# Gate/up products of a decoder layer: two more k tiles by seven products in most groups, one weight sum made by adding transfers, one partial product put into a PSUM bank

## The chip, the cores and the metric

The kernel runs on one core of a Trainium2 chip. The metric is device time in microseconds from the first to the last instruction of one execution. Several executions are timed and the median is given.

## The reference

One decoder layer on 256 tokens with 2048 channels, all in float32: a SwiGLU feed-forward block (FFN) at half weight, a token mixer (latent attention beside differential attention, merged by gates), a second such FFN, with a layer norm after each. What the change touches is the first half of both FFNs, the gate and up products:

```python
D_MODEL, SEQ, D_FF = 2048, 256, 5632
def _swiglu(x, w_gate, w_up, w_down):
    return (jax.nn.silu(x @ w_gate) * (x @ w_up)) @ w_down
...
h = _layer_norm(ALPHA * h + 0.5 * _swiglu(h, ffn1_w_gate[l], ffn1_w_up[l], ffn1_w_down[l]), ln1_g[l], ln1_b[l])
mix = _mixer(h, ...)
h = _layer_norm(ALPHA * h + mix, ln2_g[l], ln2_b[l])
h = _layer_norm(ALPHA * h + 0.5 * _swiglu(h, ffn2_w_gate[l], ffn2_w_up[l], ffn2_w_down[l]), ln3_g[l], ln3_b[l])
```

## The kernel before, in words

**Products.** Every float32 operand is split into a high part (a cast to fp32r on ScalarE, line 149) and a low part (the operand less the high part, a subtraction on VectorE, line 150). A product of a 128 x 128 block of activations with a 128 x 512 block of weights is then three matmuls, high by high, high by low and low by high (`triple`, lines 202 to 204), into one PSUM bank of 128 x 512.

**Units.** Weights stream from HBM in tiles of 128 x 1024, which hold two k tiles (of 128 rows) by 512 columns. One tile is a *unit*: its load is issued by SyncE, its split is written into a pair of tiles from a ring (`next_pair`), and its matmuls follow. `unit`, `advance` and `look` set how far these run apart: with `look(3, 4)` three units are loaded ahead of the one that is split, and four are split ahead of the one that is multiplied. The ring has six pairs in the gate/up stage (`set_ring(6)` in `second`, ten pairs before). The weights of plain units land in four rotating buffers `raw`.

**The FFN** (`ffn`, lines 705 to 821). The gate and up weights are interleaved, so that a column block of 512 holds 256 gate and 256 up columns; there are 22 such blocks, and 16 k tiles (numbered 0 to 15). The first two blocks are done by `project` with plain products (stage "projection" in this text). Then `Hybrid` does ten *groups* of two column blocks, w0 and w1, for both halves of the tokens (b = 0 and 1).

**Hybrid.** In a group the k tiles 0 to 7 are taken as a 2 x 2 matrix of blocks (tokens by k tiles 0-3 and 4-7, and these by w0 and w1), which is multiplied by seven block products in place of eight (a Strassen-like scheme). The activation sums and their splits are made once per FFN by `Seven`. The weight sums are made in each group: `plan` names for every product the block that is loaded, the tile that is split, and the tile that is first added to it on VectorE (line 344, for products 5, 6, 7 and 4). The blocks are called "11" and "21" (w0, k tiles 0-3 and 4-7), "12" and "22" (w1). Each of the seven is two units with one bank, 6 matmuls a unit. The k tiles 8 to 15 are plain units, four for each column block, 12 matmuls a unit (`plain`). The products go into banks X, Z, Y, W; what several outputs share is copied out by ScalarE in between (`after`, n1 to n3 and q5, tiles `snap`) and added or subtracted by VectorE at the end of an output (`sum_done`, line 728), followed by SiLU on ScalarE (line 715) and the gate product on VectorE (line 719). The order of units in a group is written out by hand: product 1, a plain unit, 5, plain, 6, plain, 7, plain, 2, plain, 4, plain, 3, plain, plain.

**After a group**, two units later (`later(2, ...)`), `turn_out` transposes the rows of h in blocks on VectorE (line 606), and GpSimd issues the stores (line 608) and later the loads (`get_h`, line 736) of the turned rows for the down product, done by `Sliced`.

**What sets the order.** Each engine works through a queue of its own in order. A scheduler at build time turns the program into these queues by priorities and its own estimate of times, and places tiles into slots as they come free: the large tiles (ring, `sraw`, `snap`, splits of activations) share 40 slots (`SLOTS`, tag "act"), the small ones six (`tmp_tile`). So the order of instructions on an engine need not be that of the source, and a tile that gets its slot later moves what follows. The same `Hybrid` serves the mixer with `small=True`.

Of the kernel before, what the change touches and what calls it, by code (L numbers as in the profile page):

```python
# [11 lines left out]
F32 = mybir.dt.float32  # L12
# [6 lines left out]
P = 128  # L19
# [3 lines left out]
KD = D // P  # L23
# [7 lines left out]
G = 2  # L31
SLOTS = 40
LAG = 5
# [26 lines left out]
def layer_kernel(ctx: ExitStack, tc: tile.TileContext, a: dict, out: bass.AP):  # L60
# [188 lines left out]
    class Seven:  # L249
# [35 lines left out]
        def minus(self):  # L285
# [10 lines left out]
            V.scalar_tensor_tensor(out=lo, in0=a0, scalar=-1.0, in1=hi.bitcast(F32), op0=ALU.mult, op1=ALU.subtract)  # L296

    class Hybrid:


        def __init__(self, x, seven, k_tiles, small=False):

            self.x, self.seven, self.k_tiles = x, seven, k_tiles
            self.raws = {n: [act_tile([P, 1024], F32, "sraw") for _ in range(2)] for n in ("11", "12", "22")}
            self.raws["21"] = self.raws["12"] if small else [act_tile([P, 1024], F32, "sraw") for _ in range(2)]
            self.snaps = [[act_tile([P, 2, 512], F32, "snap") for _ in range(2)] for _ in range(1 if small else 2)]
            self.last = (3, 2, 4) if small else (2, 4, 3)
            self.turn = 0

        def group(self, w0, w1, done):  # L310
            banks = {}
            snap = [t[:, i, :] for t in self.snaps[self.turn % len(self.snaps)] for i in range(2)]
            self.turn += 1
            n1, n2, n3, q5 = snap
            R = self.raws
# [11 lines left out]
            def bank(n):  # L327
# [3 lines left out]
                return banks[n], first  # L331

            def seventh(p, s):
                load_block, src, add, b = plan[p]
                st = {}

                def load():
                    w, j0 = blocks[load_block]
                    nc.sync.dma_start(R[load_block][s], w[j0 + s])

                def prep():
                    t = R[src][s]
                    if add is not None:
                        V.tensor_tensor(out=t, in0=t, in1=R[add[1]][s], op=ALU.add)  # L344
                    pair = next_pair()
                    split(*pair, t)
                    st["pair"] = [v.rearrange("p (g n) -> p g n", g=G) for v in pair]

                def now():
                    o, first = bank(b)  # L350
                    wh, wl = st["pair"]
                    xh, xl = self.seven.at_[p]
                    for g in range(G):
                        k = 2 * s + g
                        triple(o, xh[:, k, :], xl[:, k, :], wh[:, g, :], wl[:, g, :], first and g == 0,
                               s == 1 and g == 1 and p in stops, b in "XZ")
                    if s == 1 and p in after:
                        after[p]()
                unit(load if load_block else None, prep, now)

            def plain(n, j, last=False):
# [13 lines left out]
                def now():  # L375
                    wh, wl = st["pair"]
                    for b in range(2):
                        o, first = bank(names[b])
                        for g in range(G):
                            k = 2 * j + g  # L380
                            triple(o, self.x.at(0, k, b), self.x.at(1, k, b), wh[:, g, :], wl[:, g, :],
                                   first and g == 0, last and g == 1, n == 1)
                    if last:
                        done(1, 0, banks["Z"], n2, ALU.add)
                        done(1, 1, banks["X"], q5, ALU.add)
                unit(load, prep, now)

            end = self.k_tiles // G - 1
            for p, n, j in zip((1, 5, 6, 7) + self.last, (0, 0, 0, 0, 1, 1, 1), (4, 5, 6, 7, 4, 5, 6)):
                for s in range(2):  # L390
                    seventh(p, s)
                plain(n, j)
            plain(1, end, True)

# [310 lines left out]
    def ffn(n, x, wgu, wdn, residual, g, bt, each, first=None, between=None, nxt=None, cols=None):  # L705
# [19 lines left out]

        def sum_done(c, b, bank, snap, op):
            t = tmp_tile([P, 512], "gus")
            V.tensor_tensor(out=t, in0=bank, in1=snap, op=op)
            half(c, b, t[:, 256:512], t[:, 0:256])
# [16 lines left out]

        seven = Seven(x.raws)

        def second(j):
# [451 lines left out]

    xq = Acts(KD, "x", (0, 1))

# [117 lines left out]
```

## Time and profile before

| | |
|---|---|
| median of three runs | 1981.97 us (1980.86 to 1984.72) |
| profiled execution, first to last instruction | 1981.9 us |
| TensorE (PE) busy | 1967.9 us, 8832 instructions |
| VectorE (DVE) busy | 1770.4 us, 2089 instructions |
| ScalarE (ACT) busy | 1247.6 us |
| GpSimd (POOL) busy | 248.8 us |
| moved by DMA | 460.50 MB, mean 232 GB/s |
| of that, queue of GpSimd (q0) | 69.29 MB |

The records span the whole execution, so that the profiled execution has no time beside its span. The two gate/up stages (groups only) lie at about 50 to 490 us and 1330 to 1730 us; the down product of the first FFN follows until about 700 us, then the mixer. TensorE's busy times are modelled: a matmul of 512 columns is shown as 0.39 us, but the next starts 0.226 us after it. For the same reason the duration of an instruction on VectorE is longer than the distance to the next one. "DMA share" in a table by windows is the mean busy share of the 16 DMA engines, "idle before" the time in which an engine had nothing to run, with the instruction that ended it behind an arrow.

### The profile page before, as it was taken

Reading aid. Unit: us, or ns where it says so; the run is one execution under the profiler, and the core shown is the slowest. Engines: PE = TensorE matmul, PEld = TensorE weight load, DVE = VectorE, ACT = ScalarE, POOL = GpSimd, SP = SyncE. Lnnn points to the kernel's source line nnn. Section 1 sums busy time; section 2 is a strip of 40 time slices with the busy share of each in tenths; the row PEclk is TensorE's granted clock in tenths of the full one; section 3 lists DMA queues with packets and bytes.
Section 4 is the critical chain, followed back from the end, with each engine's and each line's share of the span. In section 5 each row is a group of like instructions: output and inputs, shape, how many; then the busy total and the mean of one; then the engine's idle time right before and its main releaser. Section 6 shows DMA issues by size and latency. Waiting matters only on the chain.

```text
span 1981.9 us, 25344 instructions
## 1 busy us (share of the span) xinstructions
PE 1967.9 (99%) x8832; PEld 1628.9 (82%) x8832; DVE 1770.4 (89%) x2089; ACT 1247.6 (63%) x1571; POOL 248.8 (13%) x463
## 2 busy tenths in 40 slices
PE   9999999999999999999999999999999999999997
PEld 7888888888888888888888888888888888888886
DVE  7999999999799889999877676799999999998986
ACT  6666666666556566666667764566666666665552
POOL 0111101012010011002223130001011100121000
PEclk9999999999999999999999999999999999999999
DMA  8667766658678666677667667657676666596763
GB/s 323 220 212 237 262 211 202 218 199 313 232 228 274 204 221 246 220 245 250 228 215 249 228 225 264 220 208 242 225 257 229 201 216 228 186 327 225 256 222 125
DMA packets 133649, 460.50 MB, mean 232 GB/s; under 512 B 19424, under 2 KB 19472, under 8 KB 133520
## 3 DMA queue, kind: packets, MB, share of 16 engines
q1 hardware_dynamic: 109296, 389.59, 57.4%
q0 software_dynamic: 24224, 69.29, 11.2%
q8 instruction: 69, 1.13, 0.2%
q14 instruction: 60, 0.49, 0.1%
HBM read 429.97 MB, written 28.84 MB: 231 GB/s over the span
## 4 chain that ended last, share of the span: by engine, by line
PE 90%; DVE 4%; DMA 3%; issue 2%; ACT 1%; SPq 0%; POOL 0%; DVEq 0%; ACTq 0%; POOLq 0%
PE mm L203 29%; PE mm L204 29%; PE mm L202 29%; DVE wring L150 2%; DMA raw<-in_dn_dram 1%; PE tr L203 1%; PE tr L204 1%; PE tr L202 1%; ACT wring L149 1%; DVE sraw L344 0%; PE tr L571 0%; DMA hraw<-hT 0%; DMA raw<-in_wgd_dram 0%; DMA raw<-in_gu_dram 0%; DVE sraw L519 0%
## 5 line engine op out<-in xcount | busy, mean ns | idle before, releaser
L149 ACT CAST wring<-raw 128x1024 fp32r<-128x1024 f32 (+2 forms) x499 | 516.2, 1039 | 338.7 <-PE mm L204 236.6
L150 DVE TENSOR_TENSOR wring<-raw,wring 128x1024 fp32r<-128x1024 f32 (+2 forms) x499 | 596.7, 1202 | 117.0 <-ACT wring L149 110.3
L149 ACT CAST wring<-sraw 128x1024 fp32r<-128x1024 f32 x436 | 453.7, 1052 | 217.4 <-PE mm L204 98.1
L150 DVE TENSOR_TENSOR wring<-sraw,wring 128x1024 fp32r<-128x1024 f32 x436 | 523.6, 1217 | 35.2 <-ACT wring L149 31.0
L204 PE MATMUL mm<-wring,h 128*128 128x512 f32 (+2 forms) x1296 | 499.3, 386 | 0.0
L203 PE MATMUL mm<-wring,h 128*128 128x512 f32 (+2 forms) x1296 | 498.5, 385 | 0.3 <-DVE wring L150 0.3
L202 PE MATMUL mm<-wring,h 128*128 128x512 f32 (+2 forms) x1296 | 498.6, 385 | 0.0
L203 PE MATMUL mm<-wring,xs 128*128 128x512 f32 x776 | 302.3, 390 | 0.3 <-DVE wring L150 0.3
L202 PE MATMUL mm<-wring,xs 128*128 128x512 f32 x776 | 302.5, 390 | 0.0
L204 PE MATMUL mm<-wring,xs 128*128 128x512 f32 x776 | 302.1, 389 | 0.0
L204 PEld LDWEIGHTS mm<-wring,h 128*128 128x128 f32 x1296 | 243.5, 188 | 48.9 <-DVE h L150 1.4
L202 PEld LDWEIGHTS mm<-wring,h 128*128 128x128 f32 x1296 | 243.5, 188 | 48.8 <-ACT h L149 1.0
L203 PEld LDWEIGHTS mm<-wring,h 128*128 128x128 f32 x1296 | 243.5, 188 | 48.7 <-DVE wring L150 0.9
L344 DVE TENSOR_TENSOR sraw<-sraw,sraw 128x1024 f32<-128x1024 f32 x208 | 249.9, 1211 | 1.6 <-DMA sraw<-in_gu_dram 1.5
L608 POOL DMA_DIRECT2D hT<-blocks x176 | 95.7, 551 | 766.5 <-DVE blocks L606 711.5
L203 PEld LDWEIGHTS mm<-wring,xs 128*128 128x128 f32 x776 | 145.7, 188 | 31.5 <-DVE wring L150 1.6
L202 PEld LDWEIGHTS mm<-wring,xs 128*128 128x128 f32 x776 | 145.7, 188 | 31.1 <-ACT snap L321 0.7
L204 PEld LDWEIGHTS mm<-wring,xs 128*128 128x128 f32 x776 | 145.7, 188 | 30.1
L203 PE MATMUL mm<-wring,x 128*128 128x512 f32 x384 | 149.6, 390 | 0.6 <-DVE wring L150 0.6
L202 PE MATMUL mm<-wring,x 128*128 128x512 f32 x384 | 149.5, 390 | 0.3 <-ACT wring L149 0.3
L204 PE MATMUL mm<-wring,x 128*128 128x512 f32 x384 | 149.3, 389 | 0.0
L203 PEld LDWEIGHTS mm<-wring,x 128*128 128x128 f32 x384 | 72.1, 188 | 16.2 <-DVE wring L150 1.3
(268 smaller groups left out, 1921.2 us busy)
## 6 DMA issues: line engine op xcount, KB each, us to landing
raw<-in_gu_dram SPq DMA_DIRECT2D x191, 512.0 KB, 4.4
sraw<-in_gu_dram SPq DMA_DIRECT2D x160, 512.0 KB, 5.2
raw<-in_dn_dram SPq DMA_DIRECT2D x140, 512.0 KB, 4.6
sraw<-in_dn_dram SPq DMA_DIRECT2D x36, 512.0 KB, 5.3
hraw<-hT POOLq DMA_DIRECT2D x68, 256.0 KB, 5.7
raw<-in_w_out_dram SPq DMA_DIRECT2D x32, 512.0 KB, 4.4
raw<-in_wgd_dram SPq DMA_DIRECT2D x24, 512.0 KB, 4.6
hT<-blocks POOLq DMA_DIRECT2D x176, 64.0 KB, 2.3
```

The lines of the kernel that those rows point to most:

```text
L149: S.copy(hi, src)
L150: V.tensor_tensor(out=lo, in0=src, in1=hi.bitcast(F32), op=ALU.subtract)
L202: PE.matmul(o, xh, wh, start=first, stop=False, skip_group_check=again)
L203: PE.matmul(o, xh, wl, start=False, stop=False, skip_group_check=again)
L204: PE.matmul(o, xl, wh, start=False, stop=last, skip_group_check=again)
L344: V.tensor_tensor(out=t, in0=t, in1=R[add[1]][s], op=ALU.add)
L608: nc.gpsimd.dma_start(to.rearrange("(g r) (i f) -> i r g f", g=4, i=4)[i], t[32 * i:32 * (i + 1), :].rearrange("r (g f) -> r g f", g=4))
```

## The change

Three things, all in `Hybrid` (FFNs only, not `small`):

1. In the groups p = 1, 2, 4, 5, 7, 8 and 10 of each FFN ("wide") the k tiles 8 and 9 are multiplied by the same seven products, as a 2 x 2 matrix with one k tile to a block: each product gets a third unit, half as wide (128 x 512, 3 matmuls), into the same bank, and one plain unit of either column block goes. The groups p = 3, 6 and 9 ("narrow") keep plain units there. The activation forms for it are made once per FFN (`Extra`), from a third kept quad of activations.
2. The sum for product 7, "12" + "22", is no longer an addition on VectorE. GpSimd issues a transfer that reads block "22" from HBM once more and adds it to the tile of "12".
3. Product 1 is put negated by ScalarE into the bank Y from bank X, where it lies; Y then accumulates on it, so that the output of Y needs no subtraction and no n1. The snaps are single in place of double, the order of units is a string, with another order for wide groups, and the slots are 41.

```diff
-SLOTS = 40
+SLOTS = 41
...
+    class Extra:
+        def __init__(self, x, q):
+            self.at_ = {}
+            self.x, self.q = x, q
+
+        def make(self):
+            raw = self.x.raws[self.q]
+            a0, a1, c0, c1 = (raw[:, b, i * P:(i + 1) * P] for i in range(2) for b in range(2))
+            f = tmp_tile([P, 2, 2, P], "fe")
+            fa, fb = f[:, 0], f[:, 1]
+            for out, in0, in1 in ((fa[:, 0], a1, c1), (fb[:, 0], a1, a0), (fa[:, 1], a0, fa[:, 0]), (fb[:, 1], c0, fa[:, 1])):
+                V.tensor_tensor(out=out, in0=in0, in1=in1, op=ALU.subtract)
+            t = act_tile([P, 2, 2, 2, P], F32R, "xe")
+            split(t[:, 0], t[:, 1], f)
+            for i, pair in enumerate(((5, 6), (7, 3))):
+                for m, p in enumerate(pair):
+                    self.at_[p] = [t[:, w, i, m] for w in range(2)]
+            k = 4 * self.q
+            for b, p in enumerate((2, 4)):
+                self.at_[p] = [self.x.at(w, k + 1, b) for w in range(2)]
+            t = act_tile([P, 2, P], F32R, "xm")
+            hi, lo = t[:, 0, :], t[:, 1, :]
+            S.mul(hi, a0, -1.0)
+            V.scalar_tensor_tensor(out=lo, in0=a0, scalar=-1.0, in1=hi.bitcast(F32), op0=ALU.mult, op1=ALU.subtract)
+            self.at_[1] = [hi, lo]
...
-            self.snaps = [[act_tile([P, 2, 512], F32, "snap") for _ in range(2)] for _ in range(1 if small else 2)]
-            self.last = (3, 2, 4) if small else (2, 4, 3)
-            self.turn = 0
-
-        def group(self, w0, w1, done):
+            if extra is not None:
+                for pair in (("11", "12"), ("22", "21")):
+                    t = act_tile([P, 2, 512], F32, "eraw")
+                    for i, n in enumerate(pair):
+                        self.raws[n] = self.raws[n] + [t[:, i, :]]
+            self.snaps = [act_tile([P, 2, 512], F32, "snap") for _ in range(2)]
+
+        def group(self, w0, w1, done, wide=False):
             banks = {}
-            snap = [t[:, i, :] for t in self.snaps[self.turn % len(self.snaps)] for i in range(2)]
-            self.turn += 1
-            n1, n2, n3, q5 = snap
+            small = self.small
+            n2, n3, q5, n1 = [t[:, i, :] for t in self.snaps for i in range(2)]
...
+            def begin():
+                S.mul(bank("Y")[0], banks["X"], -1.0)
+            if not small:
+                after[1] = begin
+                after[2] = lambda: done(0, 0, banks["Y"], None, None)
+
+            end_s = 2 if wide else 1
+
+            def source(name, s):
+                w, j0 = blocks[name]
+                if s < 2:
+                    return w[j0 + s]
+                i = j0 // 2
+                return w[4][:, i * 512:(i + 1) * 512]
...
                 def prep():
                     t = R[src][s]
-                    if add is not None:
+                    if add is not None and (small or p != 7):
                         V.tensor_tensor(out=t, in0=t, in1=R[add[1]][s], op=ALU.add)
-                    pair = next_pair()
+                    if not small and p == 6:
+                        nc.gpsimd.dma_start(R["12"][s], source("22", s), accum_op=ALU.add)
+                    pair = [v[:, :tiles * 512] for v in next_pair()]
                     split(*pair, t)
...
-                    for g in range(G):
-                        k = 2 * s + g
-                        triple(o, xh[:, k, :], xl[:, k, :], wh[:, g, :], wl[:, g, :], first and g == 0,
-                               s == 1 and g == 1 and p in stops, b in "XZ")
+                    for g in range(tiles):
+                        if s < 2:
+                            xh, xl = (v[:, 2 * s + g, :] for v in self.seven.at_[p])
+                        else:
+                            xh, xl = self.extra.at_[p]
+                        triple(o, xh, xl, wh[:, g, :], wl[:, g, :], first and g == 0,
+                               s == end_s and g == tiles - 1 and p in stops, b in "XZ" or not small)
...
-            for p, n, j in zip((1, 5, 6, 7) + self.last, (0, 0, 0, 0, 1, 1, 1), (4, 5, 6, 7, 4, 5, 6)):
-                for s in range(2):
-                    seventh(p, s)
-                plain(n, j)
-            plain(1, end, True)
+            if small:
+                order = "1p5p6p7p3q2q4qq"
+            elif wide:
+                order = "15p6pp72q4q3q"
+            else:
+                order = "15p6pp7p2q4q3qq"
+            turn = {n: iter(range(5 if wide else 4, end + 1)) for n in range(2)}
+            for i, c in enumerate(order):
+                if c in "pq":
+                    plain("pq".index(c), next(turn["pq".index(c)]), i == len(order) - 1)
+                else:
+                    for s in range(end_s + 1):
+                        seventh(int(c), s)
...
         def sum_done(c, b, bank, snap, op):
+            if snap is None:
+                gu_done(c, b, bank)
+                return
...
         seven = Seven(x.raws)
+        extra = Extra(x, 2)
...
-                for i, f in enumerate(seven.steps):
+                for i, f in enumerate(seven.steps + [extra.make]):
                     later(2 * i + 1, f)
...
-        hy = Hybrid(x, seven, KD)
+        hy = Hybrid(x, seven, KD, extra=extra)
...
-                     lambda n, b, bank, snap, op, p=p: sum_done(2 * p + n, b, bank, snap, op))
+                     lambda n, b, bank, snap, op, p=p: sum_done(2 * p + n, b, bank, snap, op), p % 3 != 0)
...
-    xq = Acts(KD, "x", (0, 1))
+    xq = Acts(KD, "x", (0, 1, 2))
...
-    h2 = Acts(KD, "h2", (0, 1))
+    h2 = Acts(KD, "h2", (0, 1, 2))
```

In the strings a digit is a product with all its units, p a plain unit of w0 and q one of w1.

More of the change, by code (lines that the diff above doesn't have):

```diff
@@ L298, in layer_kernel, with __init__ @@
     class Hybrid:
-        def __init__(self, x, seven, k_tiles, small=False):
-            self.x, self.seven, self.k_tiles = x, seven, k_tiles
+        def __init__(self, x, seven, k_tiles, small=False, extra=None):
+            self.x, self.seven, self.k_tiles, self.small, self.extra = x, seven, k_tiles, small, extra
             self.raws = {n: [act_tile([P, 1024], F32, "sraw") for _ in range(2)] for n in ("11", "12", "22")}
             self.raws["21"] = self.raws["12"] if small else [act_tile([P, 1024], F32, "sraw") for _ in range(2)]
-            self.snaps = [[act_tile([P, 2, 512], F32, "snap") for _ in range(2)] for _ in range(1 if small else 2)]
-            self.last = (3, 2, 4) if small else (2, 4, 3)
-            self.turn = 0
@@ L335, in seventh @@
                 st = {}
+                tiles = G if s < 2 else 1
                 def load():
-                    w, j0 = blocks[load_block]
-                    nc.sync.dma_start(R[load_block][s], w[j0 + s])
+                    nc.sync.dma_start(R[load_block][s], source(load_block, s))
                 def prep():
                     t = R[src][s]
-                    if add is not None:
+                    if add is not None and (small or p != 7):
                         V.tensor_tensor(out=t, in0=t, in1=R[add[1]][s], op=ALU.add)
-                    pair = next_pair()
+                    if not small and p == 6:
+                        nc.gpsimd.dma_start(R["12"][s], source("22", s), accum_op=ALU.add)
+                    pair = [v[:, :tiles * 512] for v in next_pair()]
                     split(*pair, t)
-                    st["pair"] = [v.rearrange("p (g n) -> p g n", g=G) for v in pair]
+                    st["pair"] = [v.rearrange("p (g n) -> p g n", g=tiles) for v in pair]
                 def now():
@@ L351, in now @@
                     wh, wl = st["pair"]
-                    xh, xl = self.seven.at_[p]
-                    for g in range(G):
-                        k = 2 * s + g
-                        triple(o, xh[:, k, :], xl[:, k, :], wh[:, g, :], wl[:, g, :], first and g == 0,
-                               s == 1 and g == 1 and p in stops, b in "XZ")
-                    if s == 1 and p in after:
+                    for g in range(tiles):
[5 more added lines that the diff above has]
+                               s == end_s and g == tiles - 1 and p in stops, b in "XZ" or not small)
+                    if s == end_s and p in after:
                         after[p]()
@@ L381, in now @@
                             triple(o, self.x.at(0, k, b), self.x.at(1, k, b), wh[:, g, :], wl[:, g, :],
-                                   first and g == 0, last and g == 1, n == 1)
+                                   first and g == 0, last and g == 1, n == 1 or not small)
                     if last:
```

## The prediction

> **What bounds the kernel now.** I read the page's engine shares, then the chain of work that ended last, then the gate/up stages in windows, because the change lies in them alone (about 50 to 490 us and 1330 to 1730 us).
>
> ```profile
> PE 1967.9 (99%) x8832; PEld 1628.9 (82%) x8832; DVE 1770.4 (89%) x2089; ACT 1247.6 (63%) x1571; POOL 248.8 (13%) x463
> ...
> PE 90%; DVE 4%; DMA 3%; issue 2%; ACT 1%; SPq 0%; POOL 0%; DVEq 0%; ACTq 0%; POOLq 0%
> ```
>
> TensorE is busy 99% of the span and holds 90% of the chain: the kernel is as long as its list of matmuls. The windows say how close the others are (columns: length, then busy us and count of PE, PEld, DVE, ACT, POOL, then clock, DMA share, GB/s).
>
> ```profile
> 200.00:300.00 100.00, 100.00 (x443) 82.81 (x442) 97.57 (x103) 64.97 (x78) 10.92 (x20) 1.00 0.67 229
> ...
> 1500.00:1600.00 100.00, 100.00 (x443) 82.81 (x442) 98.39 (x99) 68.00 (x80) 14.52 (x27) 1.00 0.69 229
> ```
>
> TensorE starts a matmul every 100.00/443 = 0.2257 us and never waits, at the full granted clock. But VectorE is busy 97.6 to 98.4%: in this stage there are two nearly full engines, and work moved from one to the other has almost no room. ScalarE (65%) and GpSimd (11%) have.
>
> What one VectorE instruction really takes is the distance of two starts where the second did not wait:
>
> ```profile
> 249.36 1.21 DVE L150 TENSOR_TENSOR wring<-sraw,wring 128x1024 fp32r<-128x1024 f32 x1
> 250.49 1.21 DVE L150 TENSOR_TENSOR wring<-raw,wring 128x1024 fp32r<-128x1024 f32 x1
> ...
> 255.03 0.68 DVE L728 TENSOR_TENSOR gus<-mm,snap 128x512 f32<-128x512 f32 x1
> 255.63 1.21 DVE L150 TENSOR_TENSOR wring<-sraw,wring 128x1024 fp32r<-128x1024 f32 x1
> 256.77 0.41 DVE L719 TENSOR_TENSOR hb<-gus,sg 128x256 f32<-128x256 f32 x1
> 257.10 0.68 DVE L728 TENSOR_TENSOR gus<-mm,snap 128x512 f32<-128x512 f32 x1
> 257.70 1.21 DVE L150 TENSOR_TENSOR wring<-raw,wring 128x1024 fp32r<-128x1024 f32 x1
> 258.83 0.41 DVE L719 TENSOR_TENSOR hb<-gus,sg 128x256 f32<-128x256 f32 x1
> 259.17 1.29 DVE L606 STREAM_TRANSPOSE blocks<-hb 128x512 f32<-128x512 f32 x2
> 260.39 1.18 DVE L344 TENSOR_TENSOR sraw<-sraw,sraw 128x1024 f32<-128x1024 f32 x1
> ```
>
> So 1.13 us for 1024 columns, 0.60 for 512, 0.33 for 256, 0.61 for a transpose.
>
> **The change part by part: matmuls.** In a group as it is, seven products of two units with 6 matmuls and eight plain units with 12 make 84 + 96 = 180, or 40.6 us. A wide group turns two plain units (24 matmuls) into seven half units of 3 (21): 177, or 39.95 us. There are 7 wide groups in each of 2 FFNs: 14 x 3 x 0.2257 = **-9.5 us**.
>
> **VectorE's load in a group.** Before: 22 subtractions and 8 additions of 1024 columns (30 x 1.13 = 33.9), 4 sums (2.4), 4 gate products (1.3), 2 transposes (1.2): 38.8 us beside 40.6, or 96%; the window shows 97.6, since some hand-overs from ScalarE add to it. Wide: 20 + 6 full (29.4), 7 half subtractions and 3 half additions (6.0), 3 sums (1.8), 1.3, 1.2: 39.7 beside 39.95. Narrow (3 of 10): 22 + 6 full (31.6), 1.8, 1.3, 1.2: 35.9 beside 40.6. The additions of product 7 and one sum that are taken away therefore pay for the half units on average, but within a wide group VectorE is at 99.4%, and with the hand-overs that the window shows (1.6 of 100) at 40.4 us beside 39.95: 0.4 us too late in each. The lead should absorb that, but a wide group also puts its VectorE work in lumps. From its last plain unit over products 1 and 5 it is 1.13 + 3.1 (two sums, gate products, transposes) + 2.9 + 5.7 = 12.8 us beside 42 matmuls = 9.5 us, and with the next plain unit and product 6 the arrears are 4.1 us. The ring holds six pairs, of which four may be prepared ahead, about 4 to 5 us of matmuls here. I take the 0.4 us as lost in the 12 wide groups that aren't first in their stage: **+5 us** (from 0, if the narrow groups pay for all, to 14 x 1 = 14, if ScalarE's hand-overs are late as well).
>
> **The start of the stage.** This is the part that the diff does not show. In the built order of the kernels ScalarE has these rows at the end of the second projection (first FFN, by the tiles that are cast):
>
> ```
> before: raw_73, sraw_76, sraw_77, raw_88, sraw_76, SiLU(60), sraw_77, sraw_76, SiLU(61), raw_89, ...
> after:  raw_73, SiLU(60), xe, xm, SiLU(61), sraw_79, sraw_80, eraw_87, raw_91, ...
> ```
>
> A name is the cast of a weight tile, and raw_73 is the projection's last; 60 and 61 are its banks. Before, six casts for the first group stand ahead of the second SiLU, now none.
>
> The loads that feed them are moved too: SyncE issued the first two sraw loads ahead of four raw loads, now it issues them behind four, each of which waits for VectorE to give back a raw buffer. ScalarE's queue is in order and a SiLU waits for its projection's last matmul; so all that was prepared behind that wait now begins only after it. The second FFN has the same order.
>
> ```profile
> 38.47 1.05 ACT L149 CAST wring<-sraw 128x1024 fp32r<-128x1024 f32 x1 [0.58 <-DMA sraw<-in_gu_dram]
> ...
> 53.29 0.39 ACT L715 ACTIVATE sg<-mm 128x256 f32<-128x256 f32 x1 [0.26 <-PE mm L204]
> 53.57 1.04 ACT L149 CAST wring<-raw 128x1024 fp32r<-128x1024 f32 x1
> ```
> ```profile
> 39.55 1.23 DVE L150 TENSOR_TENSOR wring<-sraw,wring 128x1024 fp32r<-128x1024 f32 x1 [0.32 <-ACT wring L149]
> ```
> ```profile
> 30.00:50.00 20.00, 20.00 (x90) 16.57 (x89) 17.38 (x17) 11.43 (x14) 0.00 (x0) 1.00 0.96 370
> 50.00:60.00 10.00, 10.00 (x46) 8.29 (x45) 10.00 (x12) 6.40 (x8) 4.52 (x8) 1.00 0.35 94
> 1310.00:1330.00 20.00, 20.00 (x90) 16.48 (x89) 16.41 (x17) 10.02 (x12) 0.54 (x1) 1.00 0.92 340
> 1330.00:1340.00 10.00, 10.00 (x46) 8.29 (x45) 10.00 (x12) 6.46 (x8) 2.08 (x4) 1.00 0.30 96
> ```
>
> Before, TensorE loses nothing there (20.00 and 10.00 busy). After, count from the projection's last matmul: SiLU at 0.26, cast at 0.54 (53.57 - 53.29 later), VectorE 1.08 behind it at 1.62 (39.55 - 38.47), done at 2.85. TensorE can do one matmul with the cast alone and needs the subtraction for the second: idle **2.7 us**. Then the ring is empty in the lumpiest place. Products 1 and 5 follow at once; VectorE's built order has product 1's three subtractions, then two full additions ahead of product 5's first subtraction, which ends at 1.62 + 2.86 + 2.26 + 1.2 = 8.0. TensorE has ended product 1's 15 matmuls at 2.9 + 14 x 0.2257 = 6.1 and can do one more: idle 1.8. The next subtraction costs 0.4, and product 6 (3 additions, a plain subtraction and its own, beside 12 matmuls) some 0.7. Together 5.6 a stage, **+11.2 us** for two. Bounds: 5.4 (only the first wait) to 16 (if a late first load adds 2 us to each).
>
> **Adding transfers.** 54 more transfers on GpSimd, product 7's sum: 20 groups x 1 MiB and 14 x 0.25 MiB. GpSimd has the time (54 x 0.55 us by the row below = 30 us in a 13% queue), and in the built order the transfers stand ahead of the h rows that wait for a transpose. The question is when they land. Between product 5's addition, which frees them, and the cast of product 7, VectorE's order has about 13 us of work in a narrow group and 18 in a wide one; less the issue and ScalarE's lead, 10 to 15 us. The nearest row is the plain 512 KB load by the same queue, z (L645):
>
> ```profile
> L645 POOL DMA_DIRECT2D z<-in_x_dram x4: 543/543/555, 471.6 to 517.8; - x4
> ...
> DMA to landing us min/median/max: 5.5/8.1/11.0
> ```
>
> I take 0, as nearest to its median; an adding one must also read what it adds to, so the other end is +40 (below).
>
> More bytes for all: 1.23 MB in 40.2 us is 31 GB/s on 229, so a DMA share of 0.76 if they cost like plain ones. The stage's start runs at 0.96 and TensorE doesn't wait, so that is hidden.
>
> [...]
>
> **Product 1 in the bank.** The copy becomes a multiplication of the same size. TensorE needs it at the first plain unit, in place of product 6; it stands ahead of ScalarE's casts for product 5, which TensorE needs earlier, so it is hidden. One sum of 0.60 us a group goes (counted). The snaps are no longer doubled; the next write of q5 comes over 6 us after its last read: nothing.
>
> **Down stage.** Its instructions are the same, but the built order differs; in the first FFN VectorE is full there:
>
> ```profile
> 580.00:590.00 10.00, 9.66 (x43) 7.66 (x43) 10.00 (x11) 5.44 (x6) 0.00 (x0) 1.00 0.46 143
> ```
>
> In the changed order two subtractions for later units stand ahead of the one that TensorE needs next, 2.3 us, and a sum ahead of another, 0.7: **+3 us** (0 to 4). The extra forms (two small batches) lie within the start's wait.
>
> **Sum:** -9.5 + 11.2 + 5 + 3 = +9.7. The span is 1981.9 us, with no time of its own around it in the records; the median of the three runs is 1981.97, so I go from that: 1991.7, rounded to **1992**.
>
> **Rivals.** (1) *Only the starts cost.* The narrow groups pay for the wide ones and the down stage is as before: -9.5 + 11.2 = +1.7, 1984. For it: 38.5 us of VectorE work beside 40.1 on average. Against: idle time of TensorE in a wide group can't be won back later. (2) *Faster: the refill is hidden.* If VectorE gets product 5's additions done during the first wait, each start costs 2.7 alone: -9.5 + 5.4 = -4.1, 1978; it decides from a loss of under 4.7 us a start with dense groups free. For it: in the trace before, VectorE does such additions early (L344 in the SiLU's wait). Against: the built order has them behind the subtractions. (3) *The adding transfers are late.* From a landing of about 11 us on, ScalarE waits in its queue for product 7's tile, with the next casts behind it, VectorE behind these, and TensorE once its 4 to 5 us are used up. At 13 us that is 1 us or so in each of 20 groups, at 15 some 2 us: +20 to +40 beyond the forecast, 2012 to 2032. For it: the plain load already reaches 11.0, and DMA is busier.
>
> **Chances.** Forecast (1986 to 2000) 0.44; rival 1 0.18; rival 2 0.16; rival 3 0.22. The range 1977 to 2018 takes in the first three and the milder half of the third. A measurement of this kernel tells about 0.2% (4 us) from no change. Faster by more: 0.13, most of rival 2 with a lower start; within: 0.19; slower: 0.68.
>
> **What would show it.** PE count 42 lower. TensorE idle at the first matmuls of each gate/up stage, 5 to 6 us, with SiLU ahead of the first sraw cast; 1 us or less at joints of wide groups; none in narrow ones. VectorE 99% in wide groups, 90% in narrow. Landing of the added sraw group on GpSimd's queue under 11 us, no ScalarE wait for it. I am wrong if TensorE is 100% busy at the starts, or if ScalarE's waits name an adding transfer.

## The result and the profile after

The changed kernel takes **1991.62 us** (median of four runs, 1991.57 to 1992.18). The kernel before took 1982.9 us in four runs on the same chip (1980.86 to 1984.72). The ratio is 1.0044, 95% interval 1.003 to 1.0058: slower by 0.4%. The profiled execution spans 1990.4 us, 8.5 more than before.

The first fence has four rows of the page of the kernel after: the engines, the two large DMA queues (packets, MB, share of 16 engines) and the chain. The second has the two queues before.

```profile
PE 1965.1 (99%) x8790; PEld 1620.4 (81%) x8790; DVE 1767.2 (89%) x2153; ACT 1263.4 (63%) x1645; POOL 297.8 (15%) x517
...
q1 hardware_dynamic: 113328, 389.60, 57.0%
q0 software_dynamic: 32000, 93.93, 18.0%
...
PE 86%; DVE 8%; issue 2%; DMA 2%; ACT 1%; SPq 0%; DVEq 0%; POOL 0%; ACTq 0%; POOLq 0%
```
```profile
q1 hardware_dynamic: 109296, 389.59, 57.4%
q0 software_dynamic: 24224, 69.29, 11.2%
```

TensorE has 42 instructions fewer, as the change says, and still the span is longer. VectorE's share of the chain went from 4 to 8%: TensorE now waits for VectorE in places where it did not. The windows of the kernel after (same columns as in the prediction) show where:

```profile
30.00:50.00 20.00, 20.00 (x90) 16.55 (x89) 9.97 (x13) 7.35 (x10) 0.00 (x0) 1.00 0.90 315
50.00:60.00 10.00, 6.72 (x26) 4.35 (x24) 9.24 (x14) 6.95 (x10) 5.96 (x10) 1.00 0.70 221
60.00:70.00 10.00, 9.43 (x38) 6.94 (x39) 10.00 (x12) 6.68 (x9) 1.20 (x2) 1.00 1.03 254
95.00:490.00 395.00, 394.44 (x1735) 324.83 (x1734) 383.95 (x425) 264.64 (x331) 76.99 (x126) 1.00 0.83 253
580.00:590.00 10.00, 10.00 (x46) 8.29 (x45) 10.00 (x12) 5.42 (x6) 0.00 (x0) 1.00 0.39 127
...
1330.00:1340.00 10.00, 7.40 (x31) 5.60 (x30) 5.68 (x11) 3.99 (x7) 2.99 (x6) 0.98 1.01 375
1340.00:1350.00 10.00, 9.46 (x34) 6.95 (x34) 9.10 (x11) 5.69 (x8) 4.05 (x6) 0.85 0.90 224
```

At 50 to 60 us TensorE starts 26 matmuls where the kernel before started 46, and at 1330 to 1340 it starts 31 instead of 46. In the window ahead (30 to 50), VectorE does 9.97 us of work instead of 17.38: what it did there before is now done after the wait. From 580 to 590 TensorE is full, where it was not before.

A busy TensorE hides short waits in such a table, since a matmul is shown longer (0.39 us) than its distance to the next (0.227). So I also summed, over each stage, the distances of two matmul starts that are over 0.245 us, each less 0.227, the usual distance:

```
TensorE's lost time, us        before   after   early forms (first experiment)
0-30                              2.1     2.4     1.0
30-95     first start             0.2     5.8     0.0
95-490    groups                  0.0     2.0     1.9
490-740   down product            2.9     1.5     1.5
740-1290  mixer                   7.0     9.6     9.3
1290-1375 second start            0.8     7.5     0.4
1375-1735 groups                  0.0     2.0     2.0
sum                              13.0    30.7    16.1
```

The sum grew by 17.7; less the 9.5 of the matmuls, that is 8.2 of the span's 8.5. Two thirds of it (12.3) lie at the two starts.

Two views of the first start of the kernel after. The first is ScalarE's timeline (start, duration, line, operation, in brackets the idle time before it):

```profile
49.08 0.38 ACT L773 ACTIVATE sg<-mm 128x256 f32<-128x256 f32 x1 [11.47 <-PE mm L204]
50.48 0.62 ACT L149 CAST xe<-fe 128x512 fp32r<-128x512 f32 x1 [1.01 <-DVE fe L312]
51.01 0.30 ACT L323 ACTIVATE xm<-xraw 128x128 fp32r<-128x128 f32 x1
51.86 0.38 ACT L773 ACTIVATE sg<-mm 128x256 f32<-128x256 f32 x1 [0.55 <-PE mm L204]
52.14 1.98 ACT L149 CAST wring<-sraw 128x1024 fp32r<-128x1024 f32 x2
```

ScalarE stood idle for 11.47 us in front of a SiLU that waits for TensorE, and the first cast of a weight tile for the first group (`wring<-sraw`) begins only behind the second SiLU. The second view is TensorE's own:

```profile
51.38 0.39 PE L204 MATMUL mm<-wring,x 128*128 128x512 f32 x1
53.23 0.49 PE L202 MATMUL mm<-wring,xs 128*128 128x512 f32 x1 [1.47 <-ACT wring L149]
54.86 0.50 PE L203 MATMUL mm<-wring,xs 128*128 128x512 f32 x1 [1.14 <-DVE wring L150]
```

Its next matmul starts 1.85 us after the start of the projection's last, where the cast is done, and the one after that 1.63 later, where VectorE has the low part.

The adding transfers came in time. This is the source-line view of the kernel after for the line that issues them (minimum, median, maximum in ns; below, who waited for them, and the landing):

```profile
L392 POOL DMA_DIRECT2D sraw<-in_gu_dram x40: 849/884/1208, 58.3 to 1704.6; - x40
L392 POOL DMA_DIRECT2D eraw<-in_gu_dram x14: 849/858/866, 60.9 to 1706.3; - x14
...
  ACT wring L149: 0.9, 1
...
DMA to landing us min/median/max: 3.6/5.5/9.3
```

ScalarE waited for one of them, 0.9 us in all (at 392 us). The prediction had named such a wait as a sign of being wrong. TensorE's two short waits that follow it come to 0.2 us, no more than at the same place of other narrow groups, so it is not the cost that was meant there (1 to 2 us in each of 20 groups).

### The profile page after: what moved, and what is told of

It reads as the page before. It is cut to its first block, busy times and chain, and to the rows that moved or that the text cites. A ratio compares the mean times of both kernels' runs of the same rounds, so it can differ in the third digit from the quotient of the medians.

```text
span 1990.4 us, 25588 instructions
## 1 busy us (share of the span) xinstructions
PE 1965.1 (99%) x8790; PEld 1620.4 (81%) x8790; DVE 1767.2 (89%) x2153; ACT 1263.4 (63%) x1645; POOL 297.8 (15%) x517
## 3 DMA queue, kind: packets, MB, share of 16 engines
q1 hardware_dynamic: 113328, 389.60, 57.0%
## 4 chain that ended last, share of the span: by engine, by line
PE 86%; DVE 8%; issue 2%; DMA 2%; ACT 1%; SPq 0%; DVEq 0%; POOL 0%; ACTq 0%; POOLq 0%
PE mm L203 28%; PE mm L204 27%; PE mm L202 27%; DVE wring L150 4%; DVE sraw L390 2%; PE tr L202 1%; PE tr L203 1%; PE tr L204 1%; DMA sraw<-in_wgm_dram 1%; DVE blocks L664 0%; DVE hb L777 0%; ACT wring L149 0%; PE tr L629 0%; DVE gus L789 0%; DMA turn<-blocks 0%
## 5 line engine op out<-in xcount | busy, mean ns | idle before, releaser
L149 ACT CAST wring<-raw 128x1024 fp32r<-128x1024 f32 (+2 forms) x471 | 486.4, 1038 | 345.4 <-PE mm L204 236.6
L150 DVE TENSOR_TENSOR wring<-raw,wring 128x1024 fp32r<-128x1024 f32 (+2 forms) x471 | 562.1, 1202 | 108.0 <-ACT wring L149 101.1
L204 PE MATMUL mm<-wring,h 128*128 128x512 f32 (+2 forms) x1254 | 483.2, 386 | 0.9 <-DVE h L150 0.9
L203 PE MATMUL mm<-wring,h 128*128 128x512 f32 (+2 forms) x1254 | 482.5, 385 | 0.3 <-DVE wring L150 0.3
L202 PE MATMUL mm<-wring,h 128*128 128x512 f32 (+2 forms) x1254 | 482.3, 385 | 0.3 <-ACT mm L365 0.2
L204 PEld LDWEIGHTS mm<-wring,h 128*128 128x128 f32 x1254 | 235.6, 188 | 48.6 <-DVE h L150 2.6
L202 PEld LDWEIGHTS mm<-wring,h 128*128 128x128 f32 x1254 | 235.6, 188 | 47.6 <-ACT h L149 1.1
L203 PEld LDWEIGHTS mm<-wring,h 128*128 128x128 f32 x1254 | 235.7, 188 | 46.7 <-DVE wring L150 0.6
L390 DVE TENSOR_TENSOR sraw<-sraw,sraw 128x1024 f32<-128x1024 f32 x168 | 203.2, 1218 | 2.2 <-DMA sraw<-in_wdq_dram 0.9
L203 PE MATMUL mm<-wring,x 128*128 128x512 f32 x342 | 133.5, 390 | 0.8 <-DVE wring L150 0.8
L202 PE MATMUL mm<-wring,x 128*128 128x512 f32 x342 | 132.3, 390 | 0.8 <-ACT wring L149 0.8
L204 PE MATMUL mm<-wring,x 128*128 128x512 f32 x342 | 133.1, 390 | 0.0
L392 POOL DMA_DIRECT2D sraw<-in_gu_dram x40 | 35.7, 899 | 524.3 <-DVE sraw L390 515.8
```

The costliest lines, as they stand in the source:

```text
L149: S.copy(hi, src)
L150: V.tensor_tensor(out=lo, in0=src, in1=hi.bitcast(F32), op=ALU.subtract)
L202: PE.matmul(o, xh, wh, start=first, stop=False, skip_group_check=again)
L203: PE.matmul(o, xh, wl, start=False, stop=False, skip_group_check=again)
L204: PE.matmul(o, xl, wh, start=False, stop=last, skip_group_check=again)
L392: nc.gpsimd.dma_start(R["12"][s], source("22", s), accum_op=ALU.add)
```

## The experiments

**The theory** after this result (A): the loss is made by the place of `extra.make`. It is a step of its own at the eleventh unit of the second projection, behind the first SiLU. Its tiles `xe` and `xm` take two of the 41 slots, all of which are used, so what is built after them (the `sraw` tiles of the first group, their loads and casts) moves behind it too, and on ScalarE's queue the casts stand behind both SiLUs. The traces show that the loads and casts moved (the first `sraw` load of this stage is issued at 39.77 us instead of 33.39; it lands 7.1 us later, at 46.9, and the first cast of such a tile starts at 52.14, behind the second SiLU); that the slots moved them is read from the kernel, and no run changes the slots alone. **Rivals:** (B) it is VectorE's density in wide groups; (C) the adding transfers' traffic.

**1. Forms early.** The forms are made at the eighth step, ahead of the first SiLU; nothing else changes.

```diff
-                for i, f in enumerate(seven.steps + [extra.make]):
+                for i, f in enumerate(seven.steps):
                     later(2 * i + 1, f)
+                later(8, extra.make)
```

> The changed kernel with one scheduling constant moved: the extra forms are made 8 steps after the hook and no longer 11, so that in the built order ScalarE has four casts for the first group ahead of the first SiLU and seven ahead of the second. Theory A (the starts of the two gate/up stages cost some 12 us): 1980 to 1983 us, TensorE's gaps at both starts under 1 us, and the half clock at the second start gone. Theory B (VectorE, dense with half units, costs it all along the wide groups): 1990 to 1992, no change. Theory C (the adding transfers' traffic): 1990 to 1992, no change.

Measured: 1979.28 us (1977.61 to 1980.71, 11 runs) beside 1983.39 of the kernel before; ratio 0.9978, interval 0.997 to 0.9987. This is 12.3 us under the changed kernel, 0.7 below theory A's range, and faster than the kernel before by 0.2%. ScalarE's timeline and a window of this kernel:

```profile
43.45 1.05 ACT L149 CAST wring<-sraw 128x1024 fp32r<-128x1024 f32 x1 [0.50 <-DMA sraw<-in_gu_dram]
44.40 0.61 ACT L149 CAST wring<-eraw 128x512 fp32r<-128x512 f32 x1
47.61 1.05 ACT L149 CAST wring<-sraw 128x1024 fp32r<-128x1024 f32 x1 [2.59 <-DVE sraw L390]
48.56 0.38 ACT L773 ACTIVATE sg<-mm 128x256 f32<-128x256 f32 x1
```
```profile
50.00:60.00 10.00, 10.00 (x45) 8.26 (x44) 9.94 (x13) 6.47 (x10) 4.32 (x8) 1.00 1.06 289
95.00:490.00 395.00, 394.44 (x1734) 324.74 (x1733) 383.15 (x426) 265.45 (x334) 74.97 (x125) 1.00 0.82 255
```

The casts stand ahead of the SiLU again, and TensorE starts 45 matmuls from 50 to 60. The row of the groups (95 to 490) is that of the changed kernel within 1 us on every engine but GpSimd. A holds; B and C fall as causes of the loss, since this kernel has the same wide groups and the same transfers.

**2. All groups narrow, forms late.** The wide groups are undone; the forms are still made, where the change makes them.

```diff
-                     ... sum_done(2 * p + n, b, bank, snap, op), p % 3 != 0)
+                     ... sum_done(2 * p + n, b, bank, snap, op), False)
```

> The changed kernel with no wide group: the forms are still made, late, the sum of product 7 is still made by adding transfers and product 1 is put into the bank, but k tiles 8 and 9 are plain everywhere, so TensorE has the matmuls of before. Theory A: the starts stay as in the changed kernel, 1993 to 1997. Theory B: the time of before, 1981 to 1984, since VectorE is at 88% in every group. Theory C: about 1990, what the transfers cost without the saved matmuls.

Measured: 1997.5 us (1996.76 to 2000.22), ratio 1.0073, interval 1.006 to 1.0085. That is 0.5 above theory A's range. With none of the half units left the kernel is slower still: no matmul is saved, and the starts are as bad (TensorE loses 6.8 and 8.6 us there). B falls.

**3. All groups narrow, forms early.** Both edits at once.

> As the run with no wide group, but with the forms made early. Theory A: the time of before, 1981 to 1984, so some 12 us less than its twin with late forms. Theory B: the same as that twin. Theory C: the same as that twin, some 8 us above before.

Measured: 1983.84 us (1983.01 to 1986.54), ratio 1.0003, interval 0.9994 to 1.0012: theory A. The second and third differ only in the place of the forms: 13.7 us. And the third differs from the first only in the wide groups: they are worth 4.6 us.

**4. Product 7's sum on VectorE.** Forms early, wide groups kept, adding transfers undone.

```diff
-                    if add is not None and (small or p != 7):
+                    if add is not None:
...
-                    if not small and p == 6:
-                        nc.gpsimd.dma_start(R["12"][s], source("22", s), accum_op=ALU.add)
```

> Forms early, wide groups as in the changed kernel, but product 7's sum is made by VectorE again and there are no adding transfers. VectorE's load by the distances of starts is then 42.6 us beside 39.95 in a wide group and 38.2 beside 40.6 in a narrow one. Theories A and B: VectorE becomes the bound in the wide groups, 1998 to 2008 (up to 2.6 us in each of 14, less the lead). Theory C: faster than its twin with adding transfers, under 1981.

Measured: 2002.01 us (2000.79 to 2003.9), ratio 1.0094, interval 1.0081 to 1.0108; 22.7 us over the first experiment and within the range of A and B. The window of the groups in this kernel:

```profile
95.00:490.00 395.00, 388.91 (x1691) 315.34 (x1690) 392.68 (x434) 255.43 (x324) 54.93 (x101) 1.00 0.64 215
```

VectorE is 99.4% busy and TensorE starts 43 matmuls fewer than in the first experiment. Half units need the additions off VectorE.

**5. Six wide groups.** Forms early, and `p % 3 != 1` for the wide ones, so that the first group of each block is narrow.

> Forms made early, and the wide groups are 2, 3, 5, 6, 8, 9 of each feed-forward block instead of 1, 2, 4, 5, 7, 8, 10: 36 matmuls fewer than in the kernel before instead of 42. Worked from the run with early forms and all groups narrow, 1983.8 us. Theory A (a wide group saves 0.68 us of TensorE and loses about 0.28 us of it at joints, whichever group it is): -8.1 + 12 x 0.28 = -4.8, 1979, as the run with early forms and seven wide groups (1979.3). Theory B (a wide group right behind the start, where the ring of split tiles is empty, is dearer than the others): 1976 to 1978, with TensorE idle less in the first two groups.

Measured: 1980.07 us (1978.72 to 1981.86), ratio 0.9983, interval 0.9974 to 0.9991. That is a microsecond above theory A's number and clear of B's. TensorE loses 0.2 us at the first start, where the first experiment, with a wide first group, loses none: once the casts stand ahead, a wide first group is not a dear one.

**6. All ten groups wide.** Forms early, `True` in place of `p % 3 != 0`.

> Forms made early and all ten groups of each block wide: 60 matmuls fewer than in the kernel before. Theory A (0.28 us a wide group at its joints, no more): 1983.8 - 13.5 + 20 x 0.28 = 1976, the fastest of all. Theory B (wide groups live on the slack that VectorE has in narrow ones; VectorE has 39.7 us of work beside 39.95 us of TensorE in a wide group, and without a narrow group in between its waits add up): the loss is 1 us or more a group, 1990 to 2000, with VectorE at 99% or more of the window from 95 to 490 us and TensorE at 98%.

Measured: 1986.66 us (1983.15 to 1988.37), ratio 1.0015, interval 1.0006 to 1.0024. Both numbers are missed: A by 11 us, B by 3. The mechanism of B is the nearer one, at half its price. Two windows of this kernel:

```profile
95.00:490.00 395.00, 392.74 (x1722) 322.01 (x1721) 390.35 (x445) 268.29 (x344) 78.21 (x128) 1.00 0.82 254
580.00:590.00 10.00, 8.17 (x35) 6.08 (x34) 10.00 (x11) 4.47 (x5) 0.00 (x0) 1.00 0.46 139
```

VectorE is 98.8% busy in the groups and TensorE 99.4% (B expected 99% or more, and 98%). TensorE's lost time there is 5.0 us a block, or 0.50 a group, against 0.28 a wide group where every third one is narrow (2.0 over 7 in the changed kernel). In the down product TensorE loses 2.1 us in one piece at 586 us, where it waits for VectorE (35 starts in the second row instead of 46), and 4.0 from 490 to 740 instead of 1.5; that VectorE enters this stage with less in hand is the reading, not a measurement. With 13.5 us saved and TensorE's lost time up from 13.7 in the third experiment to 28.6, wider is slower.

**7. Product 1's sum kept on VectorE.** Forms early, and ScalarE copies product 1's bank as before; VectorE takes it from the finished bank, 0.6 us a group.

```diff
-            if not small:
-                after[1] = begin
-                after[2] = lambda: done(0, 0, banks["Y"], None, None)
```

> Forms made early, and product 1's sum put back on VectorE: ScalarE copies the bank, and VectorE takes the copy from the finished bank, 0.6 us a group more (12 us in all), as in the kernel before. Theory A (what VectorE has too much of in a wide group stops TensorE there: 40.3 beside 39.95, 14 groups by 0.35 to 0.6): 1984 to 1988. Theory B (VectorE's slack over wide and narrow groups together, 11.85 us of idle time in each block by the window from 95 to 490 us, takes it): 1979 to 1981. Theory C (the put holds up TensorE at product 1): faster, below 1978.

Measured: 1979.61 us (1977.63 to 1981.75), ratio 0.9983, interval 0.9973 to 0.9992. The same as the first experiment: theory B. TensorE's lost time in the groups is 1.3 us a block beside 1.9 with the put, so the work added to VectorE did not show up as waiting there. Elsewhere some did: 0.9 us at the first start and 2.5 in the down product, where the first experiment has 0.0 and 1.5.

**8. Adding transfers alone.** The kernel before, and only product 7's sum by transfers.

> The kernel before, and of the change only product 7's sum by an adding transfer: 40 transfers of 512 KB that add, 20 MB more on the DMA engines and 45 us less on VectorE, the same matmuls. Theory A (TensorE sets the time, the transfers land in time, and their weight on the DMA engines is hidden): 1982 to 1984, no difference. Theory D (the heavier DMA traffic holds up loads, most of all in the mixer and at the ends of the blocks): 1986 to 1992. The time that TensorE is idle in the mixer (740 to 1290 us) is 6.4 in the kernel before and 9.4 in the changed one: if the adding transfers are what made the difference, it is over 8 here too.

Measured: 1983.32 us (1982.11 to 1984.79), ratio 0.9998, interval 0.9989 to 1.0006. No difference, as theory A has it: 40 additions off VectorE give nothing while TensorE sets the time, and 21 MB more on the queues cost nothing. Theory D's time is not met. By the sum of the table its lost time in the mixer is 8.0, beside 7.0 in the kernel before and 9.6 in the changed one, so the transfers account for at most 1 of these 2.6 us (one profile each; D's bound of 8 goes with another sum, which gave 6.4 and 9.4). In the down product it is 1.5 instead of 2.9.

**9 and 10. Every second group wide.** Through the traces of the changed kernel and of the first, fifth and sixth experiments, the longest distances of the group stage (0.35 us over the usual one) stand at one place, some 10 us into a wide group that follows a wide one: groups 2, 5, 8 with seven wide ones; 3, 6, 9 with six; 2 to 10 with all, where one of 0.75 follows in the last group. In the changed kernel the first of them is this one; the two matmuls ahead start at 107.36 and 107.59:

```profile
107.36 0.61 PE L202 MATMUL mm<-wring,x 128*128 128x512 f32 x2
108.16 0.50 PE L203 MATMUL mm<-wring,xs 128*128 128x512 f32 x1 [0.18 <-DVE wring L150]
```

The two kernels of these runs have no such pair: forms early, and `p % 2 == 0` or `p % 2 == 1`.

> Forms made early, and every second group wide: 2, 4, 6, 8, 10, so that no wide group follows a wide one; 30 matmuls fewer than in the kernel before. In the kernels run so far TensorE's lost time lies at product 6 of those wide groups that follow a wide one, 0.6 us for each such pair (2.0 us for three pairs with seven or six wide groups, 5.0 for nine pairs with ten). Theory A (a wide group behind a wide one costs, one behind a narrow one does not): no distance over 0.3 us in TensorE's starts from 95 to 490 us, lost time 0 to 0.5 us there, and 1983.8 - 6.8 = 1977, as fast as seven wide groups with three pairs (1979.3; worked out 1983.8 - 9.5 + 3.9 = 1978.2) or faster by a microsecond. Theory B (each wide group costs 0.28 us wherever it stands): 1.4 us lost in each block, 1983.8 - 6.8 + 2.8 = 1980.

> As the run before, with groups 1, 3, 5, 7, 9 wide, so that the last group is narrow and VectorE has its lead when the down product begins. Theory A (pairs cost): nothing lost in the groups, 1977. Theory B (each wide group costs 0.28 us): 1980. If the lead at the end of the groups matters, the lost time from 490 to 740 us is lower here than with groups 2, 4, 6, 8, 10 wide; it is 1.5 in most kernels, 2.9 in the kernel before.

Measured: 1978.63 us (1977.42 to 1981.21) with the even groups wide, ratio 0.9978, interval 0.9969 to 0.9987; 1980.45 us (1978.56 to 1981.61) with the odd ones, ratio 0.9984, interval 0.9975 to 0.9993. In the groups of the even kernel no distance is over 0.12 us above the usual one, and its window shows TensorE full:

```profile
95.00:490.00 395.00, 395.00 (x1740) 325.91 (x1739) 378.77 (x415) 263.53 (x329) 73.97 (x123) 1.00 0.82 253
```

What is left there is 0.7 us a block, in the narrow groups behind wide ones, and 1.0 us at the first start. The odd kernel loses 1.3 a block, in pieces of up to 0.27 us, half of it in its last group, which is narrow. So the 0.35 us pieces go with a wide group behind a wide one, as theory A has it: without such pairs there are none. But A's numbers (0 to 0.5 us lost, 1977) are met by neither kernel. The even one lies halfway between A and B, and the odd one has B's (1.4 us and 1980). A narrow group takes up most of what a wide one leaves, not all. Both lose 1.5 in the down product, all of it from 687 us on and none near 586, so there was nothing left for a narrow last group to save. By the medians the even kernel is the fastest of all, but it is not to be told from the first, fifth, seventh and tenth experiments: 30 matmuls fewer without waits are worth what 42 with them are.

## Why the prediction was right, point by point

The predicted time was 1992, and 1991.62 was measured. The prediction went from 1981.97 for the kernel before, which has 1982.9 here: the step up was put at 9.7 us and is 8.7. Its largest term was right, and two smaller misses, in the down product and in the mixer, stood against one another.

- **Matmuls, -9.5.** 42 fewer, as counted.
- **Starts, +11.2.** By the table 5.6 at the first and 6.7 at the second: 12.3. The first experiment, which undoes this alone, gains 12.3, and the second against the third gives 13.7. The mechanism is the one named, and it is shown. The shares in it were a little off. The first wait was put at 2.7; it is 1.63 + 1.41 = 3.0 (the 1.85 and 1.63 of the rows above, less a matmul each). The refill was put at 2.9; at the first start it is 5.8 - 3.0 - 0.2 (what was lost there before) = 2.6. The second start costs a further 1.6 that no step had: the granted clock fell to 0.50 for about 3.4 us (last section). Rival 2 (the refill hidden) falls.
- **Dense VectorE in wide groups, +5.** Lost time in the groups is 2.0 in each block, 4.0 in all. The place is near the one named, about 10 us into a group, behind products 1 and 5 (42 matmuls, 9.5 us). But the prediction put it at every wide group that isn't first, and it is at those that follow a wide one, three in a block at 0.46 each, with 0.1 to 0.2 in the narrow group behind each. A narrow group between pays most of it back, as the last two experiments show, and the sixth shows what happens without one. VectorE is busy 98.8% in a wide group (218 to 259 us), as expected, but 95.5% in the narrow one behind it (259 to 299), where 90 was expected. So rival 1, which let narrow groups pay for everything, is right of the groups next to them and wrong by these 4 us.
- **Down stage, +3 (0 to 4).** This step failed: it was -1.5 (2.9 to 1.5). The order on VectorE was read as a delay, without asking how far ahead VectorE is when it gets there. By operations and tile names VectorE's order from 577 to 592 us, around the place shown in the prediction, is the same in both traces. The eighth experiment has the order of the kernel before in the down stage, with less work for VectorE in the groups ahead, and also comes to 1.5. Through the twelve kernels TensorE waits at this place only where VectorE was busiest in the groups (of the 395 us from 95 to 490): 0.6 us in the kernel before (385.2), 1.0 in the seventh experiment (387.1), 2.4 in the sixth (390.4), 2.0 in the fourth (392.7), and nothing in the eight with 384.0 or less. This fits a lead with which VectorE leaves the groups and which decides here; no run changed the lead alone. A gain had been left out of this term's bounds without a reason.
- **Mixer.** The prediction had no term for it, and 2.6 us came from it (7.0 to 9.6). Its lost time differs between kernels that share the code there: 7.0 and 8.0 in the two that keep two quads, 7.7 to 11.2 in the ten that keep three. How much of the 2.6 is a cost of the third kept quad and how much is scatter stays open.
- **Adding transfers, 0.** Right. The plain load's row (5.5, 8.1, 11.0) was the upper side: they landed at 3.6, 5.5 and 9.3. An issue took GpSimd 0.86 to 0.88 us (medians) where 0.55 was taken from the plain one; it has the time. They weigh more on the engines than plain ones: 24.64 MB more took 18.0% of 1990.4 less 11.2% of 1981.9, or 6.8% of the span, 0.28% a MB; the plain queue has 57.0% for 389.60, 0.146. That is 1.9 times as much (1.7 times by what GpSimd's own queue takes in the kernel before, 11.2% for 69.29, 0.16); why they weigh more, no run shows. In the groups the DMA share is 0.83, where the prediction worked out 0.76 for transfers that cost like plain ones. Rival 3 falls. The fourth experiment shows what these transfers are for: without them 22.7 us more.
- **Product 1 in the bank, nothing.** Right by the seventh experiment: 0.3 us between the medians, less than can be told.

Together: -9.5 + 12.3 + 4.0 - 1.5 + 2.6 + 0.3 (the first 30 us) = +8.2, beside +8.5 in the span. So the mechanism of the starts was foreseen, and the total is right in part by luck: the down stage was put 4.5 too high and the groups 1.0, the starts 1.1 too low, and the mixer (2.6) and the first 30 us (0.3) were not counted.

## What to carry to other kernels

When a step is added ahead of a stage that has no slack, look where its instructions and its tiles stand in each engine's queue: a small batch put behind a wait moved the preparation of the whole next stage behind that wait, and cost 12 us where the change without it saves 4. When two engines are nearly full, spread the heavy groups instead of widening all: here work could be moved between them only as far as lighter groups in between paid it back (TensorE lost 5.0 us a block with ten wide groups, 0.7 or 1.3 with five that alternate with narrow ones). And a term that follows from an order needs the lead of the engine at that point: in these runs the same order cost up to 2.4 us or nothing.

## What the runs showed of the hardware

At the second start of the kernel after the granted clock (the column behind the five engines) was 0.50 for about 3.4 us. Five windows of one us each:

```profile
1339.00:1340.00 1.00, 1.00 (x4) 0.83 (x5) 1.00 (x2) 0.00 (x0) 1.00 (x3) 0.83 1.03 404
1340.00:1341.00 1.00, 1.00 (x3) 0.76 (x3) 1.00 (x3) 0.14 (x1) 1.00 (x3) 0.50 1.02 401
1341.00:1342.00 1.00, 1.00 (x4) 0.76 (x3) 1.00 (x2) 1.00 (x2) 0.36 (x1) 0.50 1.05 402
1342.00:1343.00 1.00, 1.00 (x4) 0.81 (x3) 1.00 (x2) 0.85 (x1) 0.15 (x1) 0.50 0.94 342
1343.00:1344.00 1.00, 1.00 (x5) 0.81 (x5) 1.00 (x1) 0.00 (x0) 1.00 (x2) 0.96 0.20 70
```

The shortfalls are 0.17 + 0.50 + 0.50 + 0.50 + 0.04 = 1.71 us of clock, so 3.4 us at 0.50, and matmuls start 0.427 us apart. TensorE had been idle twice just before, for 1.57 and 1.46 us with one matmul between. The first start had almost the same two waits (1.63 and 1.41) and kept its clock (1.00 from 51 to 57 us). The second experiment, whose starts lose 6.8 and 8.6 us, has a mean granted clock of 0.995 to 0.997 in its five executions, beside 0.998 to 0.999 in the eleven of the third, which differs in the place of the forms alone. In the fourth experiment one wait was enough; this is TensorE's timeline there:

```profile
594.47 0.40 PE L202 MATMUL tr<-wring,xs 128*128 128x512 f32 x1
596.67 0.68 PE L203 MATMUL tr<-wring,xs 128*128 128x512 f32 x1 [1.81 <-DVE wring L150]
597.15 0.63 PE L204 MATMUL tr<-wring,xs 128*128 128x512 f32 x1
```

From the second row to the third it is 0.48 us, then 0.43, and the granted clock is 0.50 from 597 to 600 us. But one wait of this length does not always do it: in the sixth experiment TensorE waits a little longer at the same place (2.32 us between starts), and the granted clock stays whole (1.00 in the window below, and 1.00 as the mean from 490 to 740 us, beside 0.99 in the fourth):

```profile
585.79 0.50 PE L202 MATMUL tr<-wring,xs 128*128 128x512 f32 x1
588.11 0.50 PE L203 MATMUL tr<-wring,xs 128*128 128x512 f32 x1 [1.81 <-DVE wring L150]
```
```profile
588.00:589.00 1.00, 0.90 (x4) 0.76 (x5) 1.00 (x2) 0.57 (x1) 0.00 (x0) 1.00 0.77 229
```

So the length of a wait does not decide it alone: one of 2.0 us (2.20 between starts, less a matmul) was enough once, and one of 2.1 us was not in the other run. What decides it, no run here shows.
